# A hybrid decoder layer on one core: the FFN's gate and value products taken as two-by-two blocks with seven multiplications

## The chip, the cores and the metric

The kernel runs on one core of a Trainium2 chip. The time is the device time of one execution in microseconds (us), as the median of several runs. A core has TensorE (PE, matrix products; PEld is its weight load), VectorE (DVE), ScalarE (ACT), GpSimd (POOL) and SyncE (SP), each with an instruction queue of its own that runs in the written order, and 16 DMA engines that move data between memory and the on-chip buffers. PSUM is the small memory into which TensorE writes; it is used in banks of 512 float32 columns.

## The reference

One inference step of one layer for 1024 prompt tokens and 8 x 4 sample tokens, 1056 tokens in all, with a model width of 1024. A mixer (convolution branch and dilated attention branch, each with a gate) adds `mix` to x. Then comes the part that the change touches:

```
x = x + mix
hf = rms_norm(x, g_ffn)
x = x + (silu(hf @ w_ffn_gate) * (hf @ w_ffn_up)) @ w_ffn_down     # 1024 -> 2816 -> 1024
x = x + sigmoid(rms_norm(x, g_ple) @ w_ple_gate) * (p @ w_ple)
```

and a last norm. All data are float32.

## The kernel before

Activations lie with features on the 128 partitions and tokens along the free dimension, in three chunks of 352 tokens (`C`). A feature tile is 128 features: 8 of them (`KD`) make the model width, 22 (`FT`) the FFN's hidden width. To keep float32's precision, each operand of a product is split into a high part (rounded to the fast matmul type, by ScalarE) and a low part (the rest, by VectorE), and a product is three matmuls: high x high, high x low, low x high (`mm3`, lines 113 to 120). Each matmul has its own load of 128 x 128 weights.

Weights come in slabs of 8 tiles of 128 x 128 (512 KB), in the order of their use (lines 69 to 82). `stage` issues a slab's load on SP's queue into one of two rooms `wst`; `prepare` splits it into `whi` (line 101, ScalarE) and `wlo` (line 102, VectorE), two rooms each; `slab` hands out the next one with one more split ahead. Loads run two slabs ahead.

The output product of the mixer (lines 847 to 863) takes 8 slabs of `w_out`, chunks in the order 1, 2, 0; each group of 24 matmuls ends in an add with x (line 854), whose square is summed for the norm (line 812). The sums over the partitions are taken by TensorE against a column of ones (line 174), a short chain of small VectorE steps makes 1/sqrt of them, and `rT` holds it on every partition (line 823). x1 times the gain, split, is the FFN's input `hT`.

In the FFN (lines 869 to 912) the hidden tiles go in chunks of 6, 6, 5 and 5. For one hidden tile, the gate's slab is multiplied with the three token chunks, and each result goes through the norm's factor, Silu, and the factor again (lines 884 to 886); then the value's slab, whose results are multiplied with that (line 895) and split into `mh` and `ml` (line 896, by the helper at lines 123 and 124), which stay on the chip. When a chunk of hidden tiles is done, its part of the down product runs at once (line 907) and is added to x1 (line 908). x1 stays on the chip throughout. PSUM has six banks for these products. Copies of the caches from memory to memory are issued from ScalarE's queue between slabs (`pace`).

The program is laid out by a scheduler: it writes each engine's queue in a fixed order, from the order of the code, priorities (`tc.high_priority`) and its own estimate of times. On the chip an engine never skips an instruction that waits.

## Time and profile before

| | us |
|---|---|
| three runs | 1718.75, 1721.05, 1721.37 (median 1721.05) |
| span of the profiled execution | 1721.7 |
| w_out product, in the trace | about 762 to 852 |
| FFN, in the trace | about 852 to 1637 |
| VectorE busy in 860 to 1637 | 306.2 |
| ScalarE busy in 860 to 1637 | 172.7 |

Durations in the trace are from an instruction's start to its end; matmuls and VectorE instructions overlap with the one behind them, so the throughput is read from start to start.

### The profile page before, as it was taken

What the parts mean: (1) busy time and instruction counts of PE and PEld (TensorE: products, weight loads), DVE (VectorE), ACT (ScalarE), POOL (GpSimd) and SP (SyncE); (2) the same over time, 40 slices, a digit from 0 to 9 for tenths busy, and PEclk for the clock granted to TensorE, in tenths of its full rate; (3) what the DMA queues carried; (4) which work ended last, traced back from release to release, by engine and by line L of the source; (5) the groups of instructions that cost most, each with busy time, mean ns of one, the idle gap of its engine ahead of it and who ended that gap; (6) DMA issues with size and microseconds to landing.
All of it is one profiled execution on the core that took longest, in us unless ns stands there. A gap on an engine that the chain in (4) does not pass through costs nothing.

```text
span 1721.7 us, 25453 instructions
## 1 busy us (share of the span) xinstructions
PE 1660.9 (96%) x10554; PEld 1629.2 (95%) x10554; DVE 897.6 (52%) x1529; ACT 494.4 (29%) x890; POOL 182.7 (11%) x154
## 2 busy tenths in 40 slices
PE   7999999999999978799999999999999999999996
PEld 7999999999998868689999999999999999999996
DVE  7699995121225896874543323333233333337666
ACT  7211125322263225232322201221012111225552
POOL 3100000000003766460000000000000000000003
PEclk9999999999999999899999999999999999999998
DMA  8445554511203678681233323332111111111322
GB/s 306 170 136 172 184 182 156 179 48 55 70 29 116 187 262 269 205 289 50 72 107 120 99 70 99 118 115 74 50 62 37 36 52 62 39 35 51 118 87 108
DMA packets 69348, 201.14 MB, mean 117 GB/s; under 512 B 10096, under 2 KB 25264, under 8 KB 68144
## 3 DMA queue, kind: packets, MB, share of 16 engines
q1 hardware_dynamic: 66480, 153.50, 27.6%
q10 hardware_dynamic: 2752, 46.01, 8.1%
q8 instruction: 83, 1.36, 0.3%
q14 instruction: 33, 0.27, 0.1%
HBM read 171.17 MB, written 72.15 MB: 141 GB/s over the span
## 4 chain that ended last, share of the span: by engine, by line
PE 81%; DVE 6%; issue 6%; DMA 4%; POOL 1%; ACT 1%; SPq 0%; DVEq 0%; POOLq 0%; ACTq 0%
PE mm L118 26%; PE mm L120 25%; PE mm L119 25%; DVE pr L484 2%; DMA kt<-in_kg 2%; PE ps_s L707 1%; PE N L608 1%; POOL kt L466 1%; DVE oacc L487 1%; DMA ga<-gad 1%; DMA et<-gcd 1%; DVE sc L467 1%; PE misc L174 1%; POOL y L922 0%; PE ps_s L631 0%
## 5 line engine op out<-in xcount | busy, mean ns | idle before, releaser
L118 PE MATMUL mm<-hhi,whi 128*128 128x352 f32 x2480 | 807.4, 326 | 13.3 <-DVE et L770 7.7
L120 PE MATMUL mm<-hhi,wlo 128*128 128x352 f32 x2480 | 802.1, 324 | 0.0
L119 PE MATMUL mm<-hlo,whi 128*128 128x352 f32 x2480 | 799.3, 322 | 0.0
L118 PEld LDWEIGHTS mm<-hhi,whi 128*128 128x128 f32 x2480 | 467.2, 188 | 21.1 <-DVE et L770 10.7
L120 PEld LDWEIGHTS mm<-hhi,wlo 128*128 128x128 f32 x2480 | 468.1, 189 | 3.0 <-issue 2.7
L119 PEld LDWEIGHTS mm<-hlo,whi 128*128 128x128 f32 x2480 | 468.5, 189 | 0.6 <-issue 0.2
L101 ACT ACTIVATE whi<-wst 128x1024 fp32r<-128x1024 f32 (+2 forms) x144 | 144.0, 1001 | 463.0 <-PE mm L119 437.6
L102 DVE TENSOR_TENSOR wlo<-wst,whi 128x1024 fp32r<-128x1024 f32 (+2 forms) x144 | 168.5, 1171 | 141.9 <-ACT whi L101 140.3
L118 PE MATMUL mm<-mh,whi 128*128 128x352 f32 x592 | 190.9, 323 | 0.0
L119 PE MATMUL mm<-ml,whi 128*128 128x352 f32 x592 | 189.8, 321 | 0.0
L120 PE MATMUL mm<-mh,wlo 128*128 128x352 f32 x592 | 189.6, 320 | 0.0
L338 DVE SCALAR_TENSOR_TENSOR acc<-U,vec,acc 128x1024 f32<-128x1024 f32 x120 | 147.1, 1277 | 0.4
L908 DVE TENSOR_TENSOR x<-mm,x 128x352 f32<-128x352 f32 x96 | 50.3, 524 | 131.5 <-PE mm L120 131.3
L466 POOL TENSOR_TENSOR kt<-kt,sq 128x512 f32<-128x512 f32 x48 | 64.3, 1366 | 509.9 <-DMA sq<-scr 488.1
L922 POOL TENSOR_TENSOR y<-x,r 128x704 f32<-128x704 f32 x8 | 15.1, 1921 | 923.3 <-ACT r L823 923.3
L119 PEld LDWEIGHTS mm<-ml,whi 128*128 128x128 f32 x592 | 111.2, 188 | 0.0
L118 PEld LDWEIGHTS mm<-mh,whi 128*128 128x128 f32 x592 | 111.1, 188 | 0.0
L120 PEld LDWEIGHTS mm<-mh,wlo 128*128 128x128 f32 x592 | 111.0, 187 | 0.0
L884 DVE TENSOR_TENSOR sg<-mm,r 128x352 f32<-128x352 f32 x66 | 34.5, 524 | 121.9 <-PE mm L120 117.3
L895 DVE TENSOR_TENSOR sg<-mm,sg 128x352 f32<-128x352 f32 x66 | 34.6, 524 | 121.0 <-PE mm L120 121.0
L123 ACT ACTIVATE mh<-sg 128x352 fp32r<-128x352 f32 x66 | 32.5, 493 | 136.2 <-DVE sg L895 136.2
L885 ACT ACTIVATE sg<-sg 128x352 f32<-128x352 f32 x66 | 32.4, 493 | 136.6 <-DVE sg L884 136.3
(170 smaller groups left out, 1327.0 us busy)
## 6 DMA issues: line engine op xcount, KB each, us to landing
o_rest<-in_rest ACTq DMA_DIRECT2D x32, 768.0 KB, 4.8
wst<-in_w_in SPq DMA_DIRECT2D x42, 512.0 KB, 4.8
kt<-in_kg SPq DMA_DIRECT2D x48, 256.0 KB, 3.9
kt<-in_vg SPq DMA_DIRECT2D x48, 256.0 KB, 3.1
wst<-in_w_fg SPq DMA_DIRECT2D x22, 512.0 KB, 3.5
wst<-in_w_fu SPq DMA_DIRECT2D x22, 512.0 KB, 3.6
x<-in_x SPq DMA_DIRECT2D x24, 352.0 KB, 7.2
gad<-et SPq DMA_DIRECT2D x16, 528.0 KB, 4.9
```

Of the source, the lines that this page charges most:

```text
L101: last_act[0] = ac.activation(hi[:, :n, :], st[:, :n, :], AF.Copy)
L102: ve.tensor_tensor(lo[:, :n, :], st[:, :n, :], hi[:, :n, :].bitcast(F32), op=OP.subtract)
L118: te.matmul(ps, hi[:, k, :], rh, start=(i == 0), stop=False)
L119: te.matmul(ps, hi[:, k, :], rl, start=False, stop=False)
L120: te.matmul(ps, lo[:, k, :], rh, start=False, stop=(i == n - 1))
L123: ac.activation(hi, x, AF.Copy)
L338: ve.scalar_tensor_tensor(acc[:, ct, :TP], U[:, ct, j:j + TP], vcol(w0 + j), acc[:, ct, :TP], op0=OP.mult, op1=OP.add)
L466: gp.tensor_tensor(kt, kt, st["q"][:, None, :].to_broadcast([128, n, 64]), op=OP.mult)
L484: ve.tensor_reduce(pr, vt.rearrange("p n d -> p d n"), axis=AX, op=OP.add)
L884: ve.tensor_tensor(sg, ps[:, :C], rT[c], op=OP.mult)
L895: ve.tensor_tensor(sgs[c], ps[:, :C], sgs[c], op=OP.mult)
L908: ve.tensor_tensor(x1[c][:, m], ps[:, :C], x1[c][:, m], op=OP.add)
```

## The change

The gate's and value's slabs of one hidden tile are taken as a two-by-two block matrix: A11 and A12 are the gate's weights for features 0 to 3 and 4 to 7, A21 and A22 the value's. The 1056 tokens are four quarters of 264 (`Q`), taken as two sets (`NS`) of two; for a set, B11 and B12 are features 0 to 3 of its two quarters, B21 and B22 features 4 to 7. The block product, 8 multiplications of blocks, is written with 7 (`STEPS`: M1, M5, M6, M3, M7, M2, M4) by sums of blocks.

- The weights' sums are made per hidden tile (lines 149 and 143/144 of the new file: `ws` a sum of 128 x 512, `wq` a part with its high and low half). Six rooms hold parts, so that they are made up to six steps ahead.
- The tokens' sums are made once, in place in x1, after x1 times the gain; the 7 x 2 operands `hq` (128 x 1056, split as before) stay on the chip. M1's and M5's are made during the w_out product. x1 itself is stored to memory, tile by tile, ahead of the scaling in place (line 974), and brought back during the FFN (line 1052).
- For each hidden tile and step, the two sets take 4 x 3 matmuls of 264 columns each (`mm_part`, lines 202 to 204). M6, M7 and M4 add into M1's bank, M3 into M5's; the values that stand there in between are copied or added out (lines 1025 to 1036). Norm factor, Silu, factor and product follow M2, and the last product follows M4 (line 1043).
- The hidden tile goes to memory (line 1044, from ScalarE's queue). All 22 hidden tiles are made first; then the down product runs in chunks of 6, 6, 5 and 5 as before, and loads the hidden tiles back through three staging rooms `mst` into seven rooms `mid`, where they are split (lines 207/208).

```diff
-    f = 0
+    for i in range(FT):
+        order += [(I["w_fg"][i], 8, "pair"), (I["w_fu"][i], 8, "pair")]
     for fc, nf in enumerate(F_CHUNKS):
-        for i in range(f, f + nf):
-            order += [(I["w_fg"][i], 8), (I["w_fu"][i], 8)]
-        f += nf
         order += [(I["w_fd"][fc, i, :, :nf], nf) for i in range(8)]
-    order += [(I["w_pg"][i], 8, i in KEPT) for i in range(8)]
+    order += [(I["w_pg"][i], 8) + ("kept",) * (i in KEPT) for i in range(8)]
...
+        if staged and "pair" not in staged[0]:
+            st, n, *kind = staged.popleft()
+            p, b = (keep[0], len(KEPT)) if kind else (wp, 2)
...
+    STEPS = ("M1", "M5", "M6", "M3", "M7", "M2", "M4")
+    def pair_parts(px, n_pairs):
+        tags = ((wp, "whi"), (wp, "wlo"), (px, "wx"))
+        count = [0]
+        def part(x, k):
+            p, tag = tags[count[0] % 3]
+            count[0] += 1
+            t = p.tile([128, 2, k, 128], F32R, name="wq", tag=tag, bufs=2)
+            last_act[0] = ac.activation(t[:, 0], x, AF.Copy)
+            ve.tensor_tensor(t[:, 1], x, t[:, 0].bitcast(F32), op=OP.subtract)
+            return t
+        def total(a, b, op, k):
+            t = px.tile([128, k, 128], F32, name="ws", tag="ws", bufs=3)
+            ve.tensor_tensor(t, a, b, op=op)
+            return t
+        for _ in range(n_pairs):
+            (s1, n, *_), (s2, n, *_) = staged.popleft(), staged.popleft()
+            k = n // 2
+            a11, a12, a21, a22 = s1[:, :k], s1[:, k:n], s2[:, :k], s2[:, k:n]
+            yield lambda: part(a11, k)
+            sums = {}
+            def s1_():
+                sums[1] = total(a21, a22, OP.add, k)
+                return part(sums[1], k)
+            yield s1_
+            def s2_():
+                sums[2] = total(sums[1], a11, OP.subtract, k)
+                return part(sums[2], k)
+            yield s2_
+            yield lambda: part(total(a12, sums[2], OP.subtract, k), k)
+            yield lambda: part(total(a11, a21, OP.subtract, k), k)
+            yield lambda: part(a12, k)
+            def last():
+                t = part(a22, k)
+                stage()
+                stage()
+                return t
+            yield last
+    class Parts:
+        def __init__(self, px, n_pairs, ahead=5):
+            self.it, self.ahead, self.made = pair_parts(px, n_pairs), ahead, deque()
+        def make(self):
+            with tc.high_priority(offset=PRIO):
+                f = next(self.it, None)
+                if f:
+                    self.made.append(f())
+        def next(self):
+            while len(self.made) <= self.ahead:
+                n = len(self.made)
+                self.make()
+                if len(self.made) == n:
+                    break
+            return self.made.popleft()
+    def mm_part(ps, w, h, start, k):
+        for i in range(k):
+            te.matmul(ps, w[:, 0, i], h[:, 0, i], start=start and i == 0, stop=False, skip_group_check=True)
+            te.matmul(ps, w[:, 0, i], h[:, 1, i], start=False, stop=False, skip_group_check=True)
+            te.matmul(ps, w[:, 1, i], h[:, 0, i], start=False, stop=i == k - 1, skip_group_check=True)
...
+    x_d = [dram.tile([128, T], F32, name=f"xd{m}") for m in range(KD)]
+    mid_d = [dram.tile([128, T], F32, name=f"midd{f}") for f in range(FT)]
...
+    KH = KD // 2
+    B = {}
+    def blk(s, k, t):
+        o = (2 * s + t) * Q
+        return x1[:, KH * k:KH * k + KH, o:o + Q]
+    def put(j, s, x):
+        split(B[j, s][:, 0], B[j, s][:, 1], x)
+    def room(steps):
+        for j in steps:
+            for s in range(NS):
+                B[j, s] = fh.tile([128, 2, KH, Q], F32R, name="hq", tag="hq", bufs=NS * len(steps))
+    room(("M1", "M5"))
+    def sets(m, t):
+        return x1[:, m].rearrange("p (s t q) -> p s t q", s=NS, t=2)[:, :, t]
...
+            ve.tensor_tensor(x1[:, m, cs_(c)], ps[:, :C], x1[:, m, cs_(c)], op=OP.add)
+            accum_sq(lp, c, m, into=rT[:, cs_(c)])
+        sy.dma_start(x_d[m], x1[:, m])
+        ve.tensor_scalar(x1[:, m], x1[:, m], vcol(V_FFN + m), None, op0=OP.mult)
+        i = m - KH
+        if i < 0:
+            continue
+        if i < NS:
+            put("M1", i, blk(i, 0, 0))
+            ve.tensor_tensor(blk(i, 0, 0), blk(i, 0, 1), blk(i, 0, 0), op=OP.subtract)
+            put("M5", i, blk(i, 0, 0))
+        for k in {1: (0, 1), 2: (2,), 3: (3,)}.get(i, ()):
+            ve.tensor_tensor(sets(k, 0), sets(KH + k, 1), sets(k, 0), op=OP.subtract)
+            ve.tensor_tensor(sets(k, 1), sets(KH + k, 1), sets(k, 1), op=OP.subtract)
+    lq.close()
+    mix0.close()
+    hs_.close()
+    fe = f1.enter_context(pool("fe"))
+    fh = f1.enter_context(pool("fh"))
+    room(STEPS[:1:-1])
+    parts = Parts(px, FT)
+    for s in range(NS):
+        put("M6", s, blk(s, 0, 0))
+    for s in range(NS):
+        put("M3", s, blk(s, 1, 1))
+    for s in range(NS):
+        put("M7", s, blk(s, 0, 1))
+    for s in range(NS):
+        put("M2", s, blk(s, 1, 0))
+    for s in range(NS):
+        ve.tensor_tensor(blk(s, 1, 0), blk(s, 1, 0), blk(s, 0, 0), op=OP.subtract)
+        put("M4", s, blk(s, 1, 0))
...
+    for f in range(FT):
+        X, V, Z, G, U = ({} for _ in range(5))
+        for j in STEPS:
+            w = parts.next()
+            for s in range(NS):
+                if j == "M1":
+                    bank = X[s] = mmtile(mm)[:, :Q]
+                elif j == "M5":
+                    bank = V[s] = mmtile(mm)[:, :Q]
+                elif j == "M2":
+                    bank = Z[s] = mmtile(mm)[:, :Q]
+                else:
+                    bank = V[s] if j == "M3" else X[s]
+                mm_part(bank, w, B[j, s], j in ("M1", "M5", "M2"), KH)
+                if j == "M1":
+                    G[s] = fe.tile([128, 2, Q], F32, name="fg", tag="fg", bufs=3)
+                    ac.activation(G[s][:, 0], bank, AF.Copy)
+                elif j == "M5":
+                    U[s] = fe.tile([128, Q], F32, name="fu", tag="fu", bufs=3)
+                    ac.activation(U[s], bank, AF.Copy)
+                elif j == "M6":
+                    ac.activation(G[s][:, 1], bank, AF.Copy)
+                elif j == "M3":
+                    ve.tensor_tensor(G[s][:, 1], bank, G[s][:, 1], op=OP.add)
+                elif j == "M7":
+                    ve.tensor_tensor(U[s], bank, U[s], op=OP.add)
+                elif j == "M2":
+                    ve.tensor_tensor(G[s][:, 0], bank, G[s][:, 0], op=OP.add)
+                    r = rT[:, 2 * s * Q:2 * s * Q + 2 * Q].rearrange("p (t q) -> p t q", t=2)
+                    ve.tensor_tensor(G[s], G[s], r, op=OP.mult)
+                    ac.activation(G[s], G[s], AF.Silu)
+                    ve.tensor_tensor(G[s], G[s], r, op=OP.mult)
+                    ve.tensor_tensor(G[s][:, 1], G[s][:, 1], U[s], op=OP.mult)
+                else:
+                    ve.tensor_tensor(G[s][:, 0], bank, G[s][:, 0], op=OP.mult)
+                    ac.dma_start(mid_d[f][:, 2 * s * Q:2 * s * Q + 2 * Q],
+                                 G[s].rearrange("p t q -> p (t q)"))
+            if f == 0 and j == "M6":
+                sqa[:] = [rT[:, cs_(c)] for c in range(NCH)]
+                norm_done(fe, range(NCH))
+            if j in ("M5", "M7"):
+                pace(1)
+        if f < KD:
+            sy.dma_start(x1[:, f], x_d[f])
...
+    msts = [msp.tile([128, T], F32, name=f"mst{i}") for i in range(3)]
+    fp = fs.enter_context(pool("ffn", side="right"))
+    rooms = [fp.tile([128, 2, T], F32R, name=f"mid{i}") for i in range(max(F_CHUNKS) + 1)]
     nfc = len(F_CHUNKS)
+    mids = deque()
+    def mid_load(f):
+        st, mid = msts[f % len(msts)], rooms[-1 - f % len(rooms)]
+        sy.dma_start(st, mid_d[f])
+        with tc.high_priority(offset=2 * PRIO):
+            split(mid[:, 0], mid[:, 1], st)
+        mids.append((mid[:, 0], mid[:, 1]))
+    f0 = 0
     for fc, nf in enumerate(F_CHUNKS):
-        mids = []
-        for f in range(nf):
-            mh = fp.tile([128, T], F32R, name="mh", tag="mh", bufs=max(F_CHUNKS))
-            ml = fp.tile([128, T], F32R, name="ml", tag="ml", bufs=max(F_CHUNKS))
-            mids.append((mh, ml))
-            wg = slab()
-            sgs = []
-            for c in range(NCH):
-                ps = mmtile(mm)
-                mm3(ps[:, :C], wg, range(KD), pairs(hT[c]))
-                sg = fp.tile([128, C], F32, name="sg", tag="sg", bufs=4)
-                ve.tensor_tensor(sg, ps[:, :C], rT[c], op=OP.mult)
-                ac.activation(sg, sg, AF.Silu)
-                ve.tensor_tensor(sg, sg, rT[c], op=OP.mult)
-                sgs.append(sg)
-            pace(1)
-            wu = slab()
-            pace(1)
-            for c in range(NCH):
-                ps = mmtile(mm)
-                mm3(ps[:, :C], wu, range(KD), pairs(hT[c]))
-                s = slice(c * C, (c + 1) * C)
-                ve.tensor_tensor(sgs[c], ps[:, :C], sgs[c], op=OP.mult)
-                split(mh[:, s], ml[:, s], sgs[c])
+        while f0 < sum(F_CHUNKS[:fc + 1]):
+            mid_load(f0)
+            f0 += 1
         last = fc == nfc - 1
-        if last:
-            hT = [new_h() for c in range(NCH)]
         for m in range(KD):
             w = slab()
             if m % 4 == 0:
                 pace(1)
             for c in range(NCH):
-                s = slice(c * C, (c + 1) * C)
                 ps = mmtile(mm)
-                mm3(ps[:, :C], w, range(nf), [(a[:, s], b[:, s]) for a, b in mids])
-                ve.tensor_tensor(x1[c][:, m], ps[:, :C], x1[c][:, m], op=OP.add)
+                mm3(ps[:, :C], w, range(nf), [(a[:, cs_(c)], b[:, cs_(c)]) for a, b in list(mids)[:nf]])```

The order of the instructions, as the built programs have it, at three places. First VectorE in the middle of the FFN. Before, one hidden tile (`sg` are its gate results by chunk, `wlo` the next slabs' low parts, `ml` the hidden tile's low part):

```order
L884 TENSOR_TENSOR sg_9703<-mm_9678,r0_6641 128x352
L886 TENSOR_TENSOR sg_9703<-sg_9703,r0_6641 128x352
L884 TENSOR_TENSOR sg_9732<-mm_9707,r1_6642 128x352
L886 TENSOR_TENSOR sg_9732<-sg_9732,r1_6642 128x352
L884 TENSOR_TENSOR sg_9761<-mm_9736,r2_6643 128x352
L102 TENSOR_TENSOR wlo_9767<-wst_9583,whi_9766 128x1024
L886 TENSOR_TENSOR sg_9761<-sg_9761,r2_6643 128x352
L895 TENSOR_TENSOR sg_9703<-mm_9773,sg_9703 128x352
L124 TENSOR_TENSOR ml_9671<-sg_9703,mh_9670 128x352
```

Now, the part of a hidden tile from M2 to M4 (`fg` holds a set's results, `fu` its values, `wq` are weight parts of the next tile):

```order
L1036 TENSOR_TENSOR fg_9825<-mm_9977,fg_9825 128x264
L1038 TENSOR_TENSOR fg_9825<-fg_9825,r_7011 128x528
L1036 TENSOR_TENSOR fg_9840<-mm_9995,fg_9840 128x264
L1038 TENSOR_TENSOR fg_9840<-fg_9840,r_7011 128x528
L1040 TENSOR_TENSOR fg_9825<-fg_9825,r_7011 128x528
L144 TENSOR_TENSOR wq_10015<-ws_10013,wq_10015 128x512
L1041 TENSOR_TENSOR fg_9825<-fg_9825,fu_9862 128x264
L1043 TENSOR_TENSOR fg_9825<-mm_9812,fg_9825 128x264
L1040 TENSOR_TENSOR fg_9840<-fg_9840,r_7011 128x528
L144 TENSOR_TENSOR wq_10046<-wst_9845,wq_10046 128x512
L1041 TENSOR_TENSOR fg_9840<-fg_9840,fu_9877 128x264
L1043 TENSOR_TENSOR fg_9840<-mm_9827,fg_9840 128x264
```

The work on the results is bunched behind M2, and parts of the next tile's weights stand between its steps. Second, VectorE at the seam from the w_out product to the FFN. Before, from the last add of chunk 2 on (`hlo` is the FFN's input):

```order
L854 TENSOR_TENSOR x1_2_6640<-mm_7691,x1_2_6640 128x352
L812 TENSOR_TENSOR sqa_7020<-sqa_7020,sqt_7688 128x352
L129 SCALAR_TENSOR_TENSOR hlo_7752<-x1_1_6639,vec_71,hhi_7751 128x352
L129 SCALAR_TENSOR_TENSOR hlo_7770<-x1_2_6640,vec_71,hhi_7769 128x352 x5
L854 TENSOR_TENSOR x1_0_6638<-mm_7720,x1_0_6638 128x352
L129 SCALAR_TENSOR_TENSOR hlo_7770<-x1_2_6640,vec_71,hhi_7769 128x352 x2
```

Now, from the last add on (lines 975, 984 and 985 are the scaling and two of the sums in place; `hq_7820` and `hq_7821` are M6's operands):

```order
L971 TENSOR_TENSOR x1_7010<-mm_7770,x1_7010 128x352
L144 TENSOR_TENSOR wq_7859<-ws_7857,wq_7859 128x512
L144 TENSOR_TENSOR wq_7864<-ws_7862,wq_7864 128x512
L894 TENSOR_TENSOR r_7011<-r_7011,sqt_7796 128x352
L975 TENSOR_SCALAR x1_7010<-x1_7010,vec_71 128x1056
L144 TENSOR_TENSOR wq_7900<-wst_7619,wq_7900 128x512
L984 TENSOR_TENSOR x1_7010<-x1_7010 128x2x264
L985 TENSOR_TENSOR x1_7010<-x1_7010 128x2x264
L208 TENSOR_TENSOR hq_7820<-x1_7010,hq_7820 128x1056
L262 TENSOR_SCALAR nv_7977<-misc_7967 128x9
L208 TENSOR_TENSOR hq_7821<-x1_7010,hq_7821 128x1056
```

The operands of five of the seven steps are now made behind the last add, one after the other, with weight parts and the norm's steps between them. Third, TensorE where the down product begins. Before, its first rows stand behind the last value product of six hidden tiles and take one chunk's sum over all of them:

```order
L120 MATMUL mm_8925<-hhi_7769,wlo_8769 128x352
L118 MATMUL mm_8960<-mh_7831,whi_8862 128x352
L119 MATMUL mm_8960<-ml_7832,whi_8862 128x352
L120 MATMUL mm_8960<-mh_7831,wlo_8863 128x352
L118 MATMUL mm_8960<-mh_8018,whi_8862 128x352
```

Now they stand behind the last of all M4 products (`mid6` and `mid5` are rooms of the first two hidden tiles, `mm_13145`, `mm_13165` and `mm_13185` the three chunks' sums):

```order
L204 MATMUL mm_12892<-hq_7813,wq_12907 128x264
L119 MATMUL mm_13145<-mid6_13114,whi_13133 128x352
L119 MATMUL mm_13165<-mid6_13114,whi_13133 128x352
L119 MATMUL mm_13185<-mid6_13114,whi_13133 128x352
L120 MATMUL mm_13145<-mid6_13114,whi_13133 128x352
L121 MATMUL mm_13145<-mid6_13114,wlo_13134 128x352
L119 MATMUL mm_13145<-mid5_13113,whi_13133 128x352
L120 MATMUL mm_13165<-mid6_13114,whi_13133 128x352
```

The three chunks are interleaved by hidden tile. Up to the w_out product the two programs' orders are the same.

More of the change, by code (lines that the diff above doesn't have):

```diff
@@ L40 @@
 PRIO = 300
+Q = 264
+NS = 2
 KEPT = (2, 3, 4, 5, 6)
@@ L777, in hybrid_layer @@
     evs.close()
-    xp1 = ctx.enter_context(pool("x1"))
-    x1 = [xp1.tile([128, KD, C], F32, name=f"x1_{c}") for c in range(NCH)]
-    rT = [xp1.tile([128, C], F32, name=f"r{c}") for c in range(NCH)]
     mm = ctx.enter_context(tc.tile_pool(name="mm3", bufs=6, space=PSUM, reuse_waits="tile"))
-    late = ExitStack()
-    lp = late.enter_context(pool("late"))
     ga_dma = [None]
@@ L796, in ga_load, with cs_, accum_sq @@
         return t
-    ga_next = ga_load(0, 0)
     sqa = [None] * NCH
-    def accum_sq(p, c, m, end=False, at=None):
-        x = x1[c][:, m if at is None else at]
+    def cs_(c):
+        return slice(c * C, (c + 1) * C)
+    def accum_sq(p, c, m, end=False, at=None, into=None):
+        x = x1[:, m if at is None else at, cs_(c)]
         if m == 0:
-            sqa[c] = p.tile([128, C], F32, name="sqa", tag="sqa", bufs=3)
+            sqa[c] = p.tile([128, C], F32, name="sqa", tag="sqa", bufs=3) if into is None else into
             ac.activation(sqa[c], x, AF.Square)
@@ L812, in accum_sq, with to_input @@
                 ve.tensor_tensor(sqa[c], sqa[c], t, op=OP.add)
-    def to_input(p, c, m, gain):
-        accum_sq(p, c, m)
+    def to_input(p, c, m, gain, into):
+        accum_sq(p, c, m, into=into)
         hi, lo = hT[c]
-        split_gain(hi[:, m], lo[:, m], x1[c][:, m], vcol(gain + m))
+        split_gain(hi[:, m], lo[:, m], x1[:, m, cs_(c)], vcol(gain + m))
     def norm_done(p, cs):
@@ L822, in norm_done @@
         for i, c in enumerate(cs):
-            ac.activation(rT[c], rstd_rows(cols, i), AF.Copy)
-    mixes = [(lp.tile([128, KD, C], F32R, name="mh"), lp.tile([128, KD, C], F32R, name="ml")),
+            ac.activation(rT[:, cs_(c)], rstd_rows(cols, i), AF.Copy)
+    mix0 = ExitStack()
+    lm = mix0.enter_context(pool("mix0"))
+    mixes = [(lm.tile([128, KD, C], F32R, name="mh"), lm.tile([128, KD, C], F32R, name="ml")),
              new_h(), new_h()]
+    late = ExitStack()
+    lp = late.enter_context(pool("late"))
+    ga_next = ga_load(0, 0)
     for m in range(KD):
@@ L838, in hybrid_layer @@
             split(mixes[c][0][:, m], mixes[c][1][:, m], ga[:, 0])
+    os_.close()
+    late.close()
+    xp1 = ctx.enter_context(pool("x1", side="right"))
+    x1 = xp1.tile([128, KD, T], F32, name="x1")
+    rT = xp1.tile([128, T], F32, name="r")
+    f1 = ExitStack()
+    fh = f1.enter_context(pool("fh0", side="right"))
+    px = f1.enter_context(pool("wx", side="right"))
+    KH = KD // 2
[12 more added lines that the diff above has]
+        return x1[:, m].rearrange("p (s t q) -> p s t q", s=NS, t=2)[:, :, t]
+    lq = ExitStack()
+    lp = lq.enter_context(pool("lateq"))
     def x_load(m):
@@ L904, in hybrid_layer @@
             for c in range(NCH):
-                s = slice(c * C, (c + 1) * C)
                 ps = mmtile(mm)
-                mm3(ps[:, :C], w, range(nf), [(a[:, s], b[:, s]) for a, b in mids])
-                ve.tensor_tensor(x1[c][:, m], ps[:, :C], x1[c][:, m], op=OP.add)
+                mm3(ps[:, :C], w, range(nf), [(a[:, cs_(c)], b[:, cs_(c)]) for a, b in list(mids)[:nf]])
+                ve.tensor_tensor(x1[:, m, cs_(c)], ps[:, :C], x1[:, m, cs_(c)], op=OP.add)
                 if last:
-                    to_input(fp, c, m, V_PLE)
+                    to_input(fp, c, m, V_PLE, rT[:, cs_(c)])
+        for _ in range(nf):
+            mids.popleft()
     norm_done(fp, range(NCH))
```

38 lines of the change are left out of this document (14 added, 24 removed).

## The prediction

> **What bounds the kernel now.** I read the page first: the share of each engine, the clock, the chain.
>
> ```profile
> span 1721.7 us, 25453 instructions
> ...
> PE 1660.9 (96%) x10554; PEld 1629.2 (95%) x10554; DVE 897.6 (52%) x1529; ACT 494.4 (29%) x890; POOL 182.7 (11%) x154
> ...
> PEclk9999999999999999899999999999999999999998
> ...
> PE 81%; DVE 6%; issue 6%; DMA 4%; POOL 1%; ACT 1%; SPq 0%; DVEq 0%; POOLq 0%; ACTq 0%
> ```
>
> TensorE is busy 96% of the span and carries 81% of the chain; VectorE is half idle. Then I asked for busy time by stretch: the last 90 us of the w_out product, and the FFN from its first norm to the end of its last down product (PE, PEld, DVE, ACT, POOL with counts, then the granted clock, the DMA share, GB/s).
>
> ```profile
> 770.00:860.00 90.00, 90.00 (x573) 90.00 (x573) 42.60 (x84) 28.72 (x52) 0.00 (x0) 1.00 0.19 65
> ...
> 860.00:1637.00 777.00, 777.00 (x4889) 776.91 (x4889) 306.18 (x517) 172.69 (x285) 0.00 (x0) 1.00 0.24 76
> ```
>
> No gap and full clock throughout, also across the seam at about 852 us: 777.0 / 4889 = 0.1589 us per matmul of 352 columns. Nothing else can be late here, so what the change is worth is read from two things: how many matmuls of which width TensorE issues, and what new holes it gets. The timeline inside a down product shows what sits in one such interval, each weight load beside the matmul before it:
>
> ```profile
> 1000.05 0.32 PE L120 MATMUL mm<-mh,wlo 128*128 128x352 f32 x1
> 1000.06 0.19 PEld L118 LDWEIGHTS mm<-mh,whi 128*128 128x128 f32 x1
> 1000.21 0.32 PE L118 MATMUL mm<-mh,whi 128*128 128x352 f32 x1
> ```
>
> **The matmuls, gate and value.** Before: 22 tiles x 2 products x 3 chunks x 8 x 3 = 3168 matmuls of 352 columns, 3168 x 0.1589 = 503.4 us. After: 22 x 7 steps x 2 sets x 4 x 3 = 3696 of 264 columns (3/4 of the width). In columns that is 7/8. The down product keeps its 1776 matmuls of 352.
>
> No row has a 264-column matmul of this type, so its interval q is bounded from both sides. From below by the norm's sums (line 174), which load 128 columns of weights for a product of one column:
>
> ```profile
> 853.94 1.98 PEld L174 LDWEIGHTS misc<-ones,sqa 128*128 128x128 f32 x17
> ...
> 853.94 2.06 PE L174 MATMUL misc<-ones,sqa 128*128 128x1 f32 x18
> 855.87 0.41 PE L119 MATMUL mm<-hlo,whi 128*128 128x352 f32 x1
> ...
> L174 PEld LDWEIGHTS misc<-ones,sqa x54: 187/192/338, 853.8 to 1710.4; 128*128 128x128 f32 x54
> ```
>
> Eighteen loads with next to no product take 855.87 - 853.94 = 1.93 us, 0.107 us each: loads alone would allow q = 0.107. If load and stream overlap fully, as the rows at 1000 us suggest (load 0.01 us behind the matmul before), q follows the width: 0.1589 x 264/352 = 0.119. If they partly add, a straight line from (1 column, 0.107) to (352, 0.159) gives 0.107 + 0.052 x 263/351 = 0.146. I take 0.121, near the proportional value, because some fixed part of 0.159 will not shrink: 3696 x 0.121 = 447.2, a gain of **56.2 us** (at 0.107: 107.9; at 0.146: a loss of 36.2).
>
> The Trainium skill ("TensorE: Matmul & The Clock Gate", section "Back-to-back issue gap") has N/2.4 + 2.5 ns for isolated matmuls, 149 ns for 352, and the trace shows 159; by that rule 264 columns would take 112.5 ns and the gain would be 87.6 us.
>
> **Side work in a tile.** VectorE and ScalarE by shape, then places where instructions stand back to back, and one where a sum starts after its group of matmuls:
>
> ```profile
> L102 DVE TENSOR_TENSOR wlo<-wst,whi 128x1024 fp32r<-128x1024 f32 x112 | 140.0, 1251 | 136.9 <-ACT whi L101 136.9
> ...
> L884 DVE TENSOR_TENSOR sg<-mm,r 128x352 f32<-128x352 f32 x66 | 34.5, 524 | 121.9 <-PE mm L120 117.3 <-ACT r L823 4.6
> L124 DVE TENSOR_TENSOR ml<-sg,mh 128x352 fp32r<-128x352 f32 x66 | 34.5, 522 | 23.8 <-ACT mh L123 23.7
> ...
> L332 DVE TENSOR_SCALAR acc<-U,vec 128x1024 f32<-128x1024 f32 x4 | 3.2, 808 | 0.0
> ...
> L101 ACT ACTIVATE whi<-wst 128x1024 fp32r<-128x1024 f32 x112 | 118.6, 1060 | 308.1 <-PE mm L119 298.9 <-issue 6.0 <-DMA wst<-in_w_pg 2.6
> ...
> L885 ACT ACTIVATE sg<-sg 128x352 f32<-128x352 f32 x66 | 32.4, 493 | 136.6 <-DVE sg L884 136.3 <-ACT whi L101 0.2
> ...
> 856.04 0.17 DVE L178 TENSOR_SCALAR nv<-misc 128x9 f32<-128x9 f32 x1 [5.36 <-PE misc L174]
> 856.24 0.17 DVE L181 TENSOR_SCALAR nv<-nv 128x9 int32<-128x9 int32 x1
> ...
> 868.92 0.96 DVE L886 TENSOR_TENSOR sg<-sg,r 128x352 f32<-128x352 f32 x2 [1.29 <-ACT sg L885]
> ...
> 1151.84 0.32 PE L118 MATMUL mm<-hhi,whi 128*128 128x352 f32 x1
> ...
> 1152.04 0.53 DVE L884 TENSOR_TENSOR sg<-mm,r 128x352 f32<-128x352 f32 x1 [1.17 <-PE mm L120]
> ...
> 1160.60 1.23 DVE L102 TENSOR_TENSOR wlo<-wst,whi 128x1024 fp32r<-128x1024 f32 x1 [0.41 <-ACT whi L101]
> 1161.74 0.52 DVE L886 TENSOR_TENSOR sg<-sg,r 128x352 f32<-128x352 f32 x1
> ```
>
> Start to start, VectorE takes 0.44 us for 352 elements (0.96 - 0.52) and 1.14 for 1024, so by the line through both 0.35 for 264, 0.61 for 512, 0.62 for 528, 1.17 for 1056. One tile in the new form: 4 weight sums and 7 low parts of 512 (6.7), 8 operations on PSUM and 2 products of 264 (3.5), 4 of 528 (2.5): 12.7 us, against 168 x 0.121 = 20.3 us of TensorE. ScalarE, by its rows (1060 and 493, line: 0.42, 0.63, 0.64): 7 x 0.63 + 6 x 0.42 + 2 x 0.64 = 8.2. Both fit, and the order leaves slack: the weight part of a step is made a whole tile ahead (six rooms), and the next tile's M1 goes to the banks of M5 and M3, not to M4's, so the long tail after M2 (two sets of sum, r, Silu, r, product) holds up no bank that TensorE wants next. I cost this at nothing; without that cover the tail is late by about 1 us a tile, 22 us in all. The evacuations that go (lines 884 to 896) were hidden too.
>
> **The start.** M1 and M5 need only features 0 to 3, and run while the rest is prepared: 4 x 12 x 0.121 = 5.8 us of cover after the last w_out matmul. M6 needs the last feature tile: its add (0.2 until it starts, as line 884 starts 0.20 behind the next group's first matmul, and 0.5), then its store to memory, because the scaling in place must wait until the store has read it.
>
> ```profile
> wst<-in_w_fg SPq DMA_DIRECT2D x22, 512.0 KB, 3.5
> ...
> gad<-et SPq DMA_DIRECT2D x16, 528.0 KB, 4.9
> ```
>
> That is 4.9 us more, to 5.7; scaling 0.8 (line 332's row), a difference of 0.6, ScalarE's half 1.1, VectorE's 1.2: M6 is ready at about 9.5 instead of 5.8. From there VectorE holds the row: between the last w_out sum and the M4 operands stand 10 operand splits and 2 differences of 1056 (14.0), the scaling and two differences (2.1), 12 weight operations (7.3), 8 sums (3.0) and 7 of the norm's small steps at 0.2 (1.4), 27.8 us and the wait of some 4 for the store, about 32, against 217 x 0.121 = 26.3 of TensorE. So TensorE lags about 6 us by M4. Behind that, eight loads that bring x1 back (528 KB each) stand on SP's queue ahead of the second weight slab of the third tile, and wait for the last reader of x1: 3 us more. I take **9**, from 3 (the norm steps and weight parts slide into gaps) to 18 (loads at 7 instead of 4 to 5 us).
>
> **The way through memory.** Each tile stores 2 x 264 KB from ScalarE's queue; behind these stand the next M1 copy and M4's weight part, with over 5 us of slack. At 24% DMA share there is room. In the down product the 22 loads wait on SP ahead of w_down slabs. Entering it, three staged tiles are split only after the last Silu, 1.17 us of VectorE each, and the next three need a staging room freed and a load of 3.5 to 4.9. TensorE interleaves the three chunks, 9 matmuls = 1.43 us per mid tile, and can start the next slab. Walked through, the sixth mid tile is ready about 10 us after the last M4, with some 7 to 8 us of work done by then: **3 us** (1 to 8). At the three later seams one mid tile is already there and three more are staged; the reload after the first freed room lands just in time: **2 us** in all (0 to 10). The 44 splits of 22 tiles replace 132 of 352, cheaper in sum.
>
> **The sum** against the profiled span (0.65 us above the median of the runs, 1721.05): 1721.7 - 56.2 + 9 + 3 + 2 = 1679.5, so **1679 us** for the median.
>
> **The rivals.** *Load and stream add* (slower, 10%): in the rows at 1000 us a load lasts 0.19 us, and the matmul starts 0.15 after its load began. If that 0.15 is a latency that bounds the interval, or half of it is, width saves little. It decides above q = (503.4 - 14) / 3696 = 0.132; at the line's 0.146 the time is 1721.7 + 36.2 + 14 = 1772. Against it: line 174's loads of the same 0.19 us (median 192 ns) follow each other at 0.107. *The fixed part vanishes* (12%): q falls halfway towards the load's floor, 0.113, 417.6 us, a gain of 85.8: 1721.7 - 85.8 + 14 = 1650. For it: of today's 0.159 the load covers only 0.107, and nothing in the trace says that the rest scales evenly. The Trainium skill's gap rule ("TensorE: Matmul & The Clock Gate", "Back-to-back issue gap"), 112.5 ns, would put the time here, at 1648; at 352 columns the trace does not agree with it. *VectorE's order paces the tiles* (12%): its queue is written once, with waits for loads and for ScalarE's halves between evacuations; 1 us a tile adds 22: 1702. Against it: 7 us of its 20 are idle. *No change to measure* (2%): q near 0.132, or all stalls at their upper ends with q at 0.126. That the matmuls are not made is excluded by the program's order.
>
> **The numbers.** The forecast has 64%, with its own range 1664 to 1697 (q 0.118 to 0.124, stalls 10 to 20). Faster by over 0.2% (3.4 us, about what a measurement of this kernel tells from no change): 64 + 12 + 12 - 1 = 87%; same 2%; slower 11%. The range leaves out at most 2 in 10: below, half of the fast rival, to 1645; above, q = 0.130 with the same stalls, 1721.7 - 503.4 + 480.5 + 14 = 1712.8, to 1712, which takes in VectorE's rival.
>
> **What would show it.** In the changed profile, between the first and last 264-column matmul: start-to-start in one group is q; 22 tiles at 20.3 us; VectorE about 60% busy. PE idle before lines 202 and 203 in the first three tiles sums to about 9 us, released by VectorE's operand splits and the loads; before the first mid matmul and at the seams about 5. Wrong would be: q above 0.130 or below 0.115, TensorE idle before line 202 in every tile, or a clock below 1.00 in that stretch.

## The result

The changed kernel takes **1679.74 us** (median of four runs, 1678.06 to 1680.9), beside 1721.21 us for the kernel before on the same chip: a ratio of 0.9766, 95% interval 0.9751 to 0.9781. A second comparison gave 0.9744 (0.973 to 0.9757). The forecast was 1679, so the sum came out; whether its terms did is the question here.

The page of the changed kernel: span, engines, clock, chain.

```profile
span 1676.8 us, 27134 instructions
...
PE 1614.6 (96%) x11082; PEld 1582.2 (94%) x11082; DVE 1044.2 (62%) x1803; ACT 578.6 (35%) x1056; POOL 184.1 (11%) x154
...
PEclk9999999999999989989999999999999999999998
...
PE 72%; issue 10%; DVE 9%; DMA 5%; POOL 2%; ACT 1%; SPq 0%; DVEq 0%; POOLq 0%; ACTq 0%
```

TensorE is as full as before, with 528 more instructions in 46.3 us less busy time; VectorE went from 52% to 62%. Busy time by stretch, in the middle of the hidden tiles and in the middle of the down product (columns as in the prediction):

```profile
900.00:1300.00 400.00, 399.88 (x3276) 399.66 (x3276) 260.35 (x485) 147.46 (x288) 0.00 (x0) 1.00 0.37 126
```

```profile
1330.00:1530.00 200.00, 200.00 (x1245) 1.00 0.24 78
```

The first row is the main reading: for 400 us TensorE has next to no gap, and 3276 matmuls make 0.1221 us each. VectorE is busy 65% of it. In the second row (TensorE alone), 1243 whole intervals make 0.1609 us for the 352 columns of the down product.

Where TensorE was not full: its waits from the end of the w_out product on.

```profile
L202 PE MATMUL mm<-hq,wq 128*128 128x264 f32 x1232 | 350.4, 285 | 1.9 <-DVE fg L1043 1.7
L203 PE MATMUL mm<-hq,wq 128*128 128x264 f32 x1232 | 350.5, 285 | 0.7 <-DVE hq L208 0.7
...
L120 PE MATMUL mm<-mid,whi 128*128 128x352 f32 x528 | 169.8, 323 | 1.6 <-DVE mid L208 1.6
...
L119 PE MATMUL mm<-mid,whi 128*128 128x352 f32 x528 | 167.7, 324 | 0.4 <-ACT mid L207 0.4
```

There are four short holes: one at an operand split in the first tile, one before M1 of the third tile, two at the entry to the down product, and none at the three later seams. The clock at the start, in 2 us steps from 850 us (TensorE's busy time and count, clock, DMA share, GB/s):

```profile
850.00:852.00 2.00, 2.00 (x19) 1.00 0.65 236
852.00:854.00 2.00, 2.00 (x12) 0.53 0.08 31
854.00:856.00 2.00, 2.00 (x11) 0.62 0.00 0
```

For 3.4 us TensorE ran at half clock, 0.22 us a matmul, right behind the norm's sums of one column: some 16 matmuls lost 0.1 us each, 1.6 us. Two further profiles of this kernel, below, don't have this stretch, and have instead one more hole of 1.3 us, at an operand split.

**The account.** The stretch from the first matmul of the attention product, just ahead of the w_out product, to the last of the down product; before, then after (minimum, median, maximum in ns, then first and last start):

```profile
L118 PE MATMUL mm<-ohi,whi x48: 318/323/642, 723.7 to 752.7; 128*128 128x352 f32 x48
...
L120 PE MATMUL mm<-mh,wlo x592: 318/322/328, 760.2 to 1605.6; 128*128 128x352 f32 x198
```

```profile
L119 PE MATMUL mm<-ohi,whi x48: 318/324/642, 721.0 to 750.1; 128*128 128x352 f32 x48
...
L121 PE MATMUL mm<-mid,wlo x528: 317/323/330, 1305.1 to 1559.9; 128*128 128x352 f32 x176
```

881.9 became 838.9: 43.0 us of the 44.9 between the two spans; the other 1.9 lie outside the change. (In these starts the w_out product of the kernel before runs from 753.8 to 845.7 and its last down product ends at 1605.7; the table ahead of the prediction, with 762 to 852 and 1637, has these stages too late, and its FFN takes in part of the product behind it.)

By terms: the kernel before took 505.4 us for its gate and value matmuls, 864 at 0.1612 in the first six hidden tiles and 2304 at 0.1589 (rows of both below); now they take 3696 x 0.1221 = 451.3, so 54.1 us are gained. The start costs 3.2 (start to start, the holes of the first four tiles exceed an interval by that) and 1.6 for the clock; the entry 2.3; the down product 3.2 (below). That leaves 43.8. The 0.8 too much is not resolved; 0.4 of it is the w_out product, whose 576 matmuls took 92.2 us and not 91.8.

### The profile page after: what moved, and what is told of

Same layout as the page of the kernel before. It is cut to its first block, busy times and chain, and to the rows that moved or that the text cites. A ratio compares the mean times of both kernels' runs of the same rounds, so it can differ in the third digit from the quotient of the medians.

```text
span 1676.8 us, 27134 instructions
## 1 busy us (share of the span) xinstructions
PE 1614.6 (96%) x11082; PEld 1582.2 (94%) x11082; DVE 1044.2 (62%) x1803; ACT 578.6 (35%) x1056; POOL 184.1 (11%) x154
## 4 chain that ended last, share of the span: by engine, by line
PE 72%; issue 10%; DVE 9%; DMA 5%; POOL 2%; ACT 1%; SPq 0%; DVEq 0%; POOLq 0%; ACTq 0%
PE mm L119 15%; PE mm L121 15%; PE mm L120 15%; PE mm L202 8%; PE mm L204 8%; PE mm L203 8%; DVE pr L570 2%; PE ps_s L793 1%; POOL kt L552 1%; DMA kt<-in_kg 1%; DVE oacc L573 1%; PE N L694 1%; DMA wst<-in_w_fg 1%; DMA et<-gcd 1%; DMA ga<-gad 1%
## 5 line engine op out<-in xcount | busy, mean ns | idle before, releaser
L119 PE MATMUL mm<-hhi,whi 128*128 128x352 f32 x1424 | 467.4, 329 | 10.9 <-DVE et L856 5.7
L121 PE MATMUL mm<-hhi,wlo 128*128 128x352 f32 x1424 | 464.3, 326 | 0.0
L120 PE MATMUL mm<-hlo,whi 128*128 128x352 f32 x1424 | 461.1, 324 | 0.0
L202 PE MATMUL mm<-hq,wq 128*128 128x264 f32 x1232 | 350.4, 285 | 1.9 <-DVE fg L1043 1.7
L203 PE MATMUL mm<-hq,wq 128*128 128x264 f32 x1232 | 350.5, 285 | 0.7 <-DVE hq L208 0.7
L204 PE MATMUL mm<-hq,wq 128*128 128x264 f32 x1232 | 350.4, 285 | 0.0
L119 PEld LDWEIGHTS mm<-hhi,whi 128*128 128x128 f32 x1424 | 269.2, 189 | 18.3 <-DVE et L856 8.2
L121 PEld LDWEIGHTS mm<-hhi,wlo 128*128 128x128 f32 x1424 | 269.7, 189 | 3.0 <-issue 2.7
L120 PEld LDWEIGHTS mm<-hlo,whi 128*128 128x128 f32 x1424 | 271.0, 190 | 0.6 <-issue 0.2
L202 PEld LDWEIGHTS mm<-hq,wq 128*128 128x128 f32 x1232 | 232.4, 189 | 2.5 <-ACT fg L1039 1.9
L203 PEld LDWEIGHTS mm<-hq,wq 128*128 128x128 f32 x1232 | 232.5, 189 | 1.1 <-DVE hq L208 1.1
L204 PEld LDWEIGHTS mm<-hq,wq 128*128 128x128 f32 x1232 | 232.1, 189 | 0.0
L102 ACT ACTIVATE whi<-wst 128x1024 fp32r<-128x1024 f32 (+2 forms) x100 | 97.3, 974 | 307.7 <-PE mm L120 294.2
L120 PE MATMUL mm<-mid,whi 128*128 128x352 f32 x528 | 169.8, 323 | 1.6 <-DVE mid L208 1.6
L121 PE MATMUL mm<-mid,wlo 128*128 128x352 f32 x528 | 168.5, 323 | 0.0
L119 PE MATMUL mm<-mid,whi 128*128 128x352 f32 x528 | 167.7, 324 | 0.4 <-ACT mid L207 0.4
L120 PEld LDWEIGHTS mm<-mid,whi 128*128 128x128 f32 x528 | 99.1, 188 | 1.9 <-DVE mid L208 1.9
## 6 DMA issues: line engine op xcount, KB each, us to landing
mst<-midd SPq DMA_DIRECT2D x22, 528.0 KB, 4.5
```

Source lines behind the costliest of these rows:

```text
L102: last_act[0] = ac.activation(hi[:, :n, :], st[:, :n, :], AF.Copy)
L119: te.matmul(ps, hi[:, k, :], rh, start=(i == 0), stop=False)
L120: te.matmul(ps, hi[:, k, :], rl, start=False, stop=False)
L121: te.matmul(ps, lo[:, k, :], rh, start=False, stop=(i == n - 1))
L202: te.matmul(ps, w[:, 0, i], h[:, 0, i], start=start and i == 0, stop=False, skip_group_check=True)
L203: te.matmul(ps, w[:, 0, i], h[:, 1, i], start=False, stop=False, skip_group_check=True)
```

## The experiments

Each is the changed kernel with one edit. The kernel before took between 1721.2 and 1723.8 us in the four comparisons, so beside each time stands a length that is read within one profile, from the first 264-column matmul to the last (line 202's first start and line 204's last); for the changed kernel:

```profile
L202 PE MATMUL mm<-hq,wq x1232: 278/284/425, 842.9 to 1301.9; 128*128 128x264 f32 x176
...
L204 PE MATMUL mm<-hq,wq x1232: 278/284/425, 843.2 to 1302.2; 128*128 128x264 f32 x176
```

459.3 us. The theory: the number of TensorE's matmuls, at an interval that goes with the width, sets the time, and the stalls are small. The rivals: VectorE's order or the weight loads pace the tiles, and the start costs much.

### Eight products

```diff
                 mm_part(bank, w, B[j, s], j in ("M1", "M5", "M2"), KH)
+                if j == "M2":
+                    mm_part(bank, w, B[j, s], True, KH)
```

> In every hidden tile the M2 products are issued twice, the second time from a cleared sum, so the output stays the same: eight products instead of seven, 22 x 24 = 528 more matmuls of 264 columns. Theory (TensorE's matmul count at the interval read from the changed trace, 0.122 us, sets the time): 528 x 0.122 = 64.4 us more than 1679.7, so 1744, 23 us above the kernel before, because eight narrow products cost more than the old wide ones. Rival (something beside TensorE, VectorE's order or the loads, paces the tiles): under 30 us more, 1680 to 1710.

Measured: 1743.7 us, ratio to the kernel before 1.012 (1.0094 to 1.0147); 848.1 to 1368.5, 520.4 us, 61.1 more than 459.3. The theory holds: 64.4, less some 3 us, because this profile's start has shorter holes (none before the third tile) and no half clock. It also says what the seven products had to win back: the kernel with eight products in the narrow form is 1.2% slower, 20 us, than the one before with its eight wide ones. Half of that is the interval: 4224 x 0.1221 is 10.3 us above 505.4.

### Half the width

```diff
-                mm_part(bank, w, B[j, s], j in ("M1", "M5", "M2"), KH)
+                n = Q // 2 if j in ("M6", "M7") else Q
+                mm_part(bank[:, :n], w, B[j, s][..., :n], j in ("M1", "M5", "M2"), KH)
```

> M6 and M7 take only the first 132 of the 264 columns (so half of two of the seven products is left out); the number of matmuls stays at 3696. 1056 matmuls are half as wide. Theory (the interval goes with the width down to the load's own 0.107): the narrow ones take 0.107, 1056 x 0.015 = 16 us less, 1664. Rival 1 (interval goes with the width alone): 0.061 each, 64 us less, 1615. Rival 2 (loads dominate already at 264): no difference within 3 us, 1677 to 1682.

Measured: 1669.64 us, ratio 0.9693 (0.967 to 0.9717); 847.7 to 1294.3, 446.6 us, 12.7 less. The same stretch by windows, and the first four narrow matmuls of a group:

```profile
900.00:1000.00 100.00, 100.00 (x842) 1.00 0.47 157
```

```profile
1000.42 0.22 PE L202 MATMUL mm<-hq,wq 128*128 128x132 f32 x1
1000.48 0.28 PE L203 MATMUL mm<-hq,wq 128*128 128x132 f32 x1
1000.59 0.27 PE L204 MATMUL mm<-hq,wq 128*128 128x132 f32 x1
1000.70 0.28 PE L202 MATMUL mm<-hq,wq 128*128 128x132 f32 x1
```

840 whole intervals in 100 us are 0.1190 on average; with 120 of a tile's 168 at 0.1221, the 48 narrow ones take 0.111. By the width alone they would take 0.061; that stands only in the first interval of a group (1000.42 to 1000.48), and the others are 0.11. So the theory holds in kind: there is a floor, near the interval of loads with next to no product (0.107 in the norm's sums, 0.111 here), and 264 columns lie 10% above it. In size it was off: 12.7 us in place of 16, since the floor is 0.111 and not 0.107. That the floor is the weight load is inferred from the two numbers being close.

### No trip of x1 through memory

```diff
-        sy.dma_start(x_d[m], x1[:, m])
...
-        if f < KD:
-            sy.dma_start(x1[:, f], x_d[f])
```

> The eight stores of x1 before the scaling in place and the eight loads that bring it back are left out (the down product then adds to what the scaling left in x1). Theory (the trip is hidden but for what the scaling waits): 1 to 3 us less, 1677 to 1679, with VectorE's wait of 2.4 us before line 975 gone and the wait of TensorE before M6 with it. Rival (the prediction's term: the start costs 9 us by the store and by the loads in front of weight slabs): 6 to 9 us less, 1671 to 1674.

Measured: 1677.91 us, ratio 0.9741 (0.9715 to 0.9768); 846.4 to 1302.4, 456.0 us, 3.3 less. The half clock of the first profile doesn't explain the difference: the changed kernel's two other profiles, without it, took 458.5 and 459.3, so the trip costs some 2.6 to 3.4 us, not 6 to 9. In the trace, the hole before the third tile fell from 1.7 to 0.1 and the one of 1.3 at an operand split is gone, while a new one of 0.9 stands in the fourth tile. The theory holds, at the upper end of its size. Stores and loads were left out together, so what each costs stays open; by the times alone the two ratios' intervals overlap.

### Weight parts made late

```diff
-    parts = Parts(px, FT)
+    parts = Parts(px, FT, 0)
```

> The weight parts of a step are made just before its matmuls in the order of the code, not up to six steps ahead. Theory (the parts made a tile ahead are the cover of the tail behind M2; without it TensorE waits about 1 us a tile): about 22 us more, 1702, with idle time of TensorE before line 202 in every tile. Rival (the scheduler's priority and the six rooms give the same lead anyway): within 3 us of 1679.7.

Measured: 1682.69 us, ratio 0.9772 (0.9748 to 0.9796); 845.6 to 1305.1, 459.5 us, 0.2 more. From 900 to 1300:

```profile
900.00:1300.00 400.00, 400.00 (x3279) 400.00 (x3278) 264.27 (x485) 147.81 (x291) 0.00 (x0) 1.00 0.38 123
```

The theory falls, the rival holds: in the tiles TensorE has no gap at all. The lead is not made by the place in the code: from the fifth tile on, a weight part is finished a median 13.0 us ahead of the first matmul of its step in both kernels (the n-th part against the n-th group of 24 matmuls). That leaves the six rooms and the scheduler's priorities. The cover that I named was not taken away by this edit, so what it is worth was not measured. The start did change: TensorE waits 2.0 us for M6's first operand and runs 6.8 us at half clock, and the hole before the third tile is gone.

### VectorE loaded more

The first kernel's edit; the second has `range(3)`:

```diff
+    idle = fe.tile([128, C], F32, name="idle")
...
+            if f and j in ("M1", "M5", "M6", "M3", "M7", "M2", "M4")[:7]:
+                for _ in range(1):
+                    ve.tensor_tensor(idle, rT[:, :C], rT[:, C:2 * C], op=OP.mult)
             if j in ("M5", "M7"):
                 pace(1)
```

> Seven more VectorE products of 128 x 352 that nobody reads in every hidden tile but the first, one after each step: 7 x 0.44 = 3.1 us of its 20.5 us, of which it is busy 13.5 now. Theory (the order leaves slack, TensorE never waits for VectorE in the tiles): at most 2 us more, 1680 to 1682. Rival (VectorE's order paces the tail behind M2, so what is put between costs): 21 x 1 to 3 us, 1700 to 1745.

> The same with three such products after each step: 21 x 0.44 = 9.2 us a tile, 22.7 in all against TensorE's 20.5. Theory: now VectorE is the bound, 21 x 2.2 = 46 us more, 1726, a point above the kernel before; TensorE waits in every tile. If it were more than 60 us, the slack in the order would be smaller than its idle time; if less than 20, the durations overlap more than read.

Measured: 1683.47 us (ratio 0.9768, 0.9752 to 0.9785; 460.8 us, 1.5 more) and 1686.67 us (0.9793, 0.9778 to 0.9807; 466.1 us, 6.8 more). The first is a little above its forecast, far from the rival's. The second is far from the 46 us, for a reason in the trace: nobody reads these products, so the scheduler was free to place them. It did not keep them at their steps in either kernel: the 147 of the first end at 1113.2 us, the 441 of the second at 1468.7, in the down product. Both fill VectorE to 90% and not beyond. The second kernel:

```profile
1000.00:1100.00 100.00, 99.84 (x820) 99.62 (x819) 90.54 (x187) 36.26 (x72) 0.00 (x0) 1.00 0.49 159
1100.00:1200.00 100.00, 99.47 (x816) 99.26 (x815) 90.77 (x188) 36.90 (x74) 0.00 (x0) 1.00 0.28 96
1200.00:1300.00 100.00, 97.25 (x782) 96.63 (x781) 90.39 (x187) 35.75 (x71) 0.00 (x0) 0.98 0.26 81
```

With VectorE at 90% instead of 65%, TensorE loses half a per cent or less, but for the last row: there one hole of 2.6 us waits for VectorE's add behind M7, with 3.4 us at half clock behind it. The rival asked for 1 us or more in every tile, so this is enough against it: some 25 us of work in 100 fit between the evacuations, and the tail behind M2 is not paced by what stands between its steps. Where VectorE does become the bound was not reached.

### Six products

```diff
-                mm_part(bank, w, B[j, s], j in ("M1", "M5", "M2"), KH)
+                if j != "M4":
+                    mm_part(bank, w, B[j, s], j in ("M1", "M5", "M2"), KH)
```

> The M4 products are left out (the last result is then made of what stands in the bank): six products a tile, 528 matmuls of 264 columns fewer. Theory (TensorE's count sets the time, and VectorE with 13.5 us a tile is still far from it): 528 x 0.122 = 64.4 us less, 1615. Rival (the next limit, VectorE's order or the weight loads, is close behind): less than 50 us gained, with TensorE idle in every tile.

Measured: 1623.78 us, ratio 0.9421 (0.9408 to 0.9434), 56.0 less than the changed kernel's 1679.79 in this comparison; 845.1 to 1246.0, 400.9 us, 58.4 less. In the tiles the theory holds to the digit:

```profile
900.00:1000.00 100.00, 100.00 (x823) 100.00 (x822) 73.41 (x142) 41.75 (x84) 0.00 (x0) 1.00 0.56 183
1000.00:1100.00 100.00, 100.00 (x823) 100.00 (x822) 77.21 (x146) 42.81 (x89) 0.00 (x0) 1.00 0.53 175
```

The missing 6 us are at the start: TensorE, with less to do in the first tiles, stands 4.7 us between the norm's transposes and the next 264-column matmul, and runs 6.8 us at half clock behind that.

### The second profiles

> The changed kernel once more, for a second profile. Theory (the two levels of the interval belong to the order of the matmuls): 0.122 in the tiles and 0.161 in the down product again. Rival (they belong to the single execution): another level, 0.120 or 0.159, in one of the two. The hole of 2 us before M1 of the third tile and the 2 us at the entry to the down product come back; the 3.4 us at half clock at 852 need not.

> The kernel before once more, for a second profile. Theory: 0.161 in the first gate products and 0.159 from the first down product on, as in the first profile. Rival: another level, chosen by the execution.

The changed kernel (1678.73 us) and the kernel before (1726.52 us), once each. TensorE in windows, first of the second profile of the changed kernel, then of the kernel before in its first and its second profile:

```profile
900.00:1300.00 400.00, 400.00 (x3279) 1.00 0.38 126
1330.00:1530.00 200.00, 200.00 (x1244) 1.00 0.25 78
```

```profile
880.00:980.00 100.00, 100.00 (x622) 1.00 0.34 111
1100.00:1500.00 400.00, 400.00 (x2519) 1.00 0.20 63
```

```profile
880.00:980.00 100.00, 100.00 (x623) 1.00 0.32 106
1100.00:1500.00 400.00, 400.00 (x2519) 1.00 0.20 63
```

400 / 2517 = 0.1589 in both profiles of the kernel before from its first down product on, 0.161 in its first gate products in both, and 0.161 in the down product of all profiles of the changed kernel. So in these profiles the level belongs to the program, not to the execution; in the kernel before it changes where the first down product begins. What sets it stays open; it is worth 1584 x 0.0020 = 3.2 us here. The stretch at half clock at 852 us did not come back; the holes did, and one more of 1.3 us, before line 203 at 855.4 us. In the first profile TensorE, slowed by the half clock, came to that matmul at 855.6 and had no wait: the two stand for each other.

### The norm on GpSimd

```diff
...
         for _ in range(3):
+            if ve is gp:
+                gp.tensor_tensor(z, y, y, op=OP.mult)
+                gp.tensor_tensor(z, z, v, op=OP.mult)
+                gp.tensor_scalar(z, z, -0.5, 1.5, op0=OP.mult, op1=OP.add)
+                gp.tensor_tensor(y, z, y, op=OP.mult)
+                continue
...
-                norm_done(fe, range(NCH))
+                norm_done(fe, range(NCH), gp)
```

> The changed kernel itself, on the chip of the three runs beside it, so that they can be compared: 0.977 of the kernel before, the hole of 1.9 us before M1 of the third tile and the one of 1.9 us in the first products of the down product as in its two profiles.

> The three Newton rounds of the FFN's norm (12 small steps in place of 9) are taken by GpSimd, which is idle there, not by VectorE behind the operands' splits. Theory (the hole of 1.9 us before M1 of the third tile comes from the late norm factor, queued on VectorE): that hole goes, the norm factor is there some 15 us earlier, 2 us less than the changed kernel. Rival (the hole comes from the x1 loads that stand ahead of the third tile's weights): it stays, no difference within 1 us.

The changed kernel: 1679.79 us, ratio 0.9744. With the norm on GpSimd: 1688.78 us, ratio 0.9797 (0.9784 to 0.981), 9.0 us slower; 846.6 to 1312.9, 466.3 us, 7.0 more. The hole before the third tile is gone, and a bigger one stands ahead of it. That doesn't show the theory: the norm factor came 12 us earlier, but line 1043's product in the first tile only 2.3, while TensorE's 289th narrow matmul, the one that had waited, started 4.5 us later (all counted from the first 264-column matmul). A late TensorE hides the hole as well. GpSimd's and TensorE's rows there:

```profile
860.22 1.10 POOL L272 TENSOR_TENSOR nv<-nv 128x9 f32<-128x9 f32 x1
861.41 1.08 POOL L273 TENSOR_SCALAR nv<-nv 128x9 f32<-128x9 f32 x1
...
868.59 0.20 POOL L274 TENSOR_TENSOR nv<-nv 128x9 f32<-128x9 f32 x1
...
868.85 1.54 PE L285 MATMUL misc<-ident,nv 128*128 128x128 f32 x6 [4.35 <-POOL nv L274]
```

```profile
868.00:870.00 2.00, 1.16 (x6) 0.50 0.00 0
870.00:872.00 2.00, 2.00 (x11) 0.50 0.00 0
872.00:874.00 2.00, 2.00 (x12) 0.61 0.00 0
```

The scheduler put the first six transposes 138 matmuls earlier into TensorE's queue, behind 110 and not 248 of the narrow products. GpSimd's steps took up to 1.1 us where VectorE was splitting operands, so TensorE waited 4.4 us, and ran at half clock behind it.

### x1 brought back later

On top of the norm on GpSimd:

```diff
+            last_dma[0] = sy.dma_start(st[:, :n, :], src)
...
-        if f < KD:
-            sy.dma_start(x1[:, f], x_d[f])
+        if 6 <= f < 6 + KD:
+            with tc.issue_after(last_dma[0].ins):
+                sy.dma_start(x1[:, f - 6], x_d[f - 6])
```

> As the run before, and x1 is brought back one tile at a time between the weight slabs of the middle of the FFN, not by eight loads in a row ahead of the third tile's weights. Theory (only the norm chain mattered): no further difference within 1 us, 2 us less than the changed kernel in all. Rival (the loads in front of weights cost too): 1 to 3 us less again, and the wait of ScalarE for a weight load of 4.1 us in the first tiles goes.

Measured: 1686.81 us, ratio 0.9785 (0.9772 to 0.9798), 2.0 less than the run before, with overlapping intervals; 844.9 to 1307.6, 462.7 us, 3.6 less in these two profiles. The holes of 0.5 to 1.3 us that the run before had at 896, 930 and 941 us are gone, and ScalarE's longest wait for a gate slab fell from 4.2 to 1.5 us. So in this form the loads ahead of weights cost some 2 to 3 us, as the rival has it; the changed kernel itself has only one hole of 0.4 there, at 920. The hole before the transposes remains, and the whole is slower than the changed kernel.

## Why the prediction was right

**The matmuls** (56.2 us expected, 54.1 measured). The step that carries the result: the interval of 264 columns, taken as 0.121 between 0.107 and 0.146, is 0.1221. Load and stream overlap, and width counts down to a floor. The rival at 0.146 and the one at 0.113 are both out. The Trainium skill ("TensorE: Matmul & The Clock Gate", "Back-to-back issue gap") has a gap rule for isolated matmuls: its 112.5 ns is 8% short here, and for 132 columns it would give 57.5 ns where the run shows 111.

Two slips stand in the prediction's readings. The 503.4 us come from 0.1589 over the window 860 to 1637, which reaches past the last down product (1605.7) and averages two levels; the matmuls took 505.4. And 1776 takes in the 192 matmuls of `mh` in w_out; the down product has 1584. No term used that count.

**Side work in a tile** (nothing expected, nothing measured). VectorE about 60% busy was forecast, 65% read, and no tile beyond the third has a hole worth naming. What was named as the cover, the six rooms, is still there in the late version, so it was not tested; the lead in the code is not needed for it.

**The start** (9 expected; 4.8, 4.1 and 4.9 in the three profiles). The step was mis-sized in two places. The store of the last feature tile landed in 2.7 us, not 4.9 (the one in this window, 840 to 900):

```profile
xd<-x SPq DMA_DIRECT2D x1, 528.0 KB, 2.7
```

And I counted the cover ahead of M6 as M1 and M5 alone, though the 18 sums of the norm stand between: 1.9 us more. M6 didn't wait; the holes of 0.7 and, without the half clock, 1.3 us stand at later operand splits. The third tile's hole of 1.7 us was there, but the profile's releaser is not a weight load: it is line 1043 of the first tile, which came late because the norm factor did. The way there, behind the factor's last small step at 874.8, in rows of three engines (the transposes, Silu's table load, Silu, line 1043):

```profile
877.87 0.82 PE L277 MATMUL misc<-ident,nv 128*128 128x128 f32 x6
...
880.86 1.28 ACT L1039 ACT_TABLE_LOAD   x1
882.15 0.65 ACT L1039 ACTIVATE fg<-fg 128x528 f32<-128x528 f32 x1
...
885.04 0.42 DVE L1043 TENSOR_TENSOR fg<-mm,fg 128x264 f32<-128x264 f32 x1
```

I had counted the twelve small steps as 1.4 us of VectorE's time, not as a chain: its links stand one by one behind VectorE's operand splits, from 850.9 to 874.8. But the chain is not all of it. The transposes didn't wait for the last step; they stand 3.1 us later in TensorE's queue, behind other products. ScalarE then waits 1.0 us for a weight load and takes 1.3 us to load a table. So the loads have a part too: without the trip of x1 line 1043's product came 3.7 us earlier and the hole was 0.1. No run separates these shares. The 1.6 us at half clock were not foreseen.

**The way through memory** (3 + 2 expected, 2.3 + 0 measured). At the entry the walk was right in kind: VectorE splits the first hidden tiles only after the last product. At the seams nothing is left.

**Not seen:** the down product at 0.161, 3.2 us. So the matmul gain came out 2 us smaller, the stalls 7 us smaller and this term 3 us larger: the sum of 1679 owes its last digits to errors that cancel, and that is luck. The order of the terms, and that TensorE's count and interval decide in the tiles, is what the runs show.

## What to carry to other kernels

When TensorE is full, count matmuls times the interval at their own width: a narrower form pays in proportion only while it stays above the floor (0.111 us here), and the form itself can cost (here 1.2%) before the saved product pays it back. Extra work on half-idle engines cost next to nothing in the middle tiles here, up to 90% of VectorE; it is the first tiles, where one chain of small steps queues behind large ones, that show what it costs. Moving such a chain to an idle engine also moved, in this scheduled program, what waits for it.
